# The kept pooled part is added to the gated output by an accumulating transfer on GpSimd's queue

## The chip, the cores and the metric

The kernel runs on one core of one Trainium2 chip. A core has five engines that run side by side and wait for each other through semaphores: TensorE (PE in the profile, with its weight loads as PEld) multiplies matrices into PSUM banks, VectorE (DVE) and ScalarE (ACT) work element by element, GpSimd (POOL) does the same without access to PSUM, and SyncE (SP) issues transfers between the chip's memory and the on-chip SBUF. Each engine runs its own instructions in a fixed order. The metric is the time of one execution on the device in microseconds. Before the change the median of three runs is 1211.2 us (1210.49 to 1212.1).

## The reference

One block of a streaming encoder on 1024 tokens of width 1024, with 16 meta tokens ahead of them, all in float32. A pooling mixer and a gated linear attention work side by side, and their outputs are merged by two sigmoid gates; an output projection and a squared-ReLU MLP follow. Cut to what matters here:

```python
def hybrid_mixer(u, ...):
    z = jnp.einsum('bld,dn->bln', u, w_in)
    a, q, k, v, r, lr, ga, gb = jnp.split(z, IN_SPLITS, axis=-1)
    ...
    y_a = jnp.einsum('blc,cd->bld', p, w_pool_out)
    ...
    y_b = jnp.einsum('blc,cd->bld', o.reshape(B, L, GLA_VAL), w_gla_out)
    m = jax.nn.sigmoid(ga) * y_a + jax.nn.sigmoid(gb) * y_b
    return jnp.einsum('bld,de->ble', m, w_out)
```

Here `p` is the multi-scale pooling of `a` and `o` the output of the linear attention. The change concerns the `+` in `m`: its left side is the pooled part, its right side the gated output of the attention.

## The kernel before

All activations are kept with channels on the 128 partitions and tokens along the free dimension. A tile of 128 channels by 512 tokens (one **half** of the sequence) is the unit of the merge. A float32 product is made of three matmuls of split operands (`mm3`, L281 to L287): each operand is a **high part** (a rounded copy, made by ACT) and a **low part** (what is left, made by DVE). Weights come in through `Raw` buffers by SP and are split the same way in a `Ring` of two slots (L84 on ACT, L85 on DVE).

The stage around the change runs from about 393 to 503 us of the span. Its products are:

- `ya_block(j)`: the pooled product for output channels d = 2j and 2j + 1, both halves. Its gate (a tanh kept in `ga_dram`) is applied by DVE at L1161, and the result is stored in `ma_dram` (L1162). This is the kept pooled part.
- `yb_block(j, h)`: the attention's product for d = 2j and 2j + 1 of half h, four k steps of three matmuls each into one of three PSUM banks (`bank("mm")`). DVE applies the gate from `gb_dram` (L1195, the **gate product**, which is the last reader of the bank) and adds the kept pooled part (L1196, the **add**). ACT writes the high part of half the sum (L1199) and DVE the low part (L1200). These are the inputs of the output projection, `out_tile` (L1362).

TensorE's order is written out by hand. In half 0 the blocks run as j = 0, 1, 2, 3, beside the attention's state work (`across`). In half 1 they run as j = 2, 3, 0, one output tile, j = 1, and then the other output tiles. The weights of j = 2 and 3 stay in the ring from half 0 to half 1 (`KEPT`). The order on DVE, ACT, SP and GpSimd is set by a planner when the kernel is built, from the dependences and from its own estimates of durations; an engine then keeps to that order.

Gates and kept parts are loaded ahead by `ask` into a circle of 128x512 buffers, the same buffers also holding the result in place. `take` hands them to a block. There are ten buffers in the first part of the stage (three of the tile `o`, three of `t1`, four of `c`, `lend("o", "t1", "c")` in `gla_open`) and eight in the second (four of a new `t1`, four of a new `o`). At most two less than all may be in flight:

```python
        while wanted and S["io_live"] < most:
            kind, d, h = wanted[0]
            drams = (ga_dram,) if kind == "a" else (gb_dram, ma_dram)
            if S["io_live"] + len(drams) > len(S["io"]) - 2:
                return
```

The second set is made in `merge_open` (L1313), which gives the first set's memory back:

```python
        left.pop_to(left_m)
        right.pop_to(1)
        S["wo"] = [left.push("wo0", [P, 2, KT, HALF], F32R)]
        ...
        buffer("t1", 4)
        buffer("o", 4)
        lend("t1", "o")
```

In the built program's memory map the old `o` lies at bytes 190336 to 196480 of a partition; the new `t1` lies at 188288 to 196480 and so covers it; the new `o` (from 196480) covers the attention's half 0 output `yg0`; and `wo0` covers the old `c` and `t1`. A tile that is placed over an older one waits until all uses of the whole older tile are over.

`wo` is the split output projection weight. Its first half is loaded into `acc` and split by L1344 (ACT) and L1345 (DVE), and the first output tile reads it.

Of the kernel before, what the change touches and what calls it, by code (L numbers as in the profile page):

```python
# [11 lines left out]
ALU = mybir.AluOpType  # L12
# [110 lines left out]
def kernel(  # L123
# [3 lines left out]
    nc = tc.nc  # L127
# [6 lines left out]
    act, dve, pool, pe = nc.scalar, nc.vector, nc.gpsimd, nc.tensor  # L134
# [19 lines left out]
    def bank(tag):  # L154
        if tag == "sc":
            sc_n[0] += 1
            return two("sc")[:, sc_n[0] % 2]
        return psp[tag].tile([P, 512], F32, name=f"b_{tag}", tag=tag)
# [10 lines left out]
    ma_dram = dp.tile([8, 2, P, HALF], F32, name="ma_dram")  # L169
    gb_dram = dp.tile([8, 2, P, HALF], F32, name="gb_dram")  # L170
    r_dram = dp.tile([HEADS, 2, P, HALF], F32, name="r_dram")
    ga_dram = dp.tile([8, 2, P, HALF], F32, name="ga_dram")
# [38 lines left out]
    def f32(ap):  # L211
        return ap.bitcast(F32)
# [68 lines left out]
    def mm3(ps, n, lhs, rhs, first=True, last=True, more=False):  # L281

        for i in range(n):
            (ah, al), (bh, bl) = lhs(i), rhs(i)
            pe.matmul(ps, ah, bh, start=first and i == 0, stop=False, skip_group_check=more)  # L285
            pe.matmul(ps, ah, bl, start=False, stop=False, skip_group_check=more)  # L286
            pe.matmul(ps, al, bh, start=False, stop=last and i == n - 1, skip_group_check=more)  # L287
# [151 lines left out]
    def first_stage(xs, us, xm, um, lrraw):  # L439
# [23 lines left out]
        def ask(i, j):  # L463
            vraw.append(raw.load(w_rows(C_V + 256 * i, 256, j), D).rearrange("p (k c) -> p k c", k=4))

        ask(0, 0)
        ask(0, 1)
        load(2)
        load(3)
# [79 lines left out]
        def low(i, j):  # L549
# [4 lines left out]
            wait=lambda i, j: W1.ask(),  # L554
            square=square, log=log, exp=exp, root=root, scale=scale, turn=turn, keep=keep, hi=hi, lo=lo, high=high,
            low=low, ask=ask, value=v_half, out=v_out, first=W1.split, meta=lambda t: transposed(um[:META], 0, 0),
        )
        for word in ORDER_1.split():
# [564 lines left out]
    def slot():  # L1123
        S["io_n"] += 1
        return S["io"][(S["io_n"] - 1) % len(S["io"])]

    def ask(most=16):

        while wanted and S["io_live"] < most:
            kind, d, h = wanted[0]  # L1130
            drams = (ga_dram,) if kind == "a" else (gb_dram, ma_dram)
            if S["io_live"] + len(drams) > len(S["io"]) - 2:
                return
            S["io_live"] += len(drams)
            have[wanted.pop(0)] = [slot() for _ in drams]
            for o, dram in zip(have[kind, d, h], drams):
                nc.sync.dma_start(o, dram[d, h])

    def take(*key):
        S["io_live"] -= len(have[key])  # L1140
        return have[key]
# [30 lines left out]
    def yb_block(j, h):  # L1172
        def fn(wb=None):
            if h and j in KEPT:
                wb = kept.pop(j)
            elif j in KEPT:
                kept[j] = wb
            hi, lo = (t.rearrange("p (k c) -> p k c", k=4) for t in wb)
            while not h and ("o", 0) not in done:
                yield "wait"  # L1180
            yg = S["yg"][h]
            for e in range(2):
                d, w = 2 * j + e, slice(e * P, (e + 1) * P)
                ask()
                gl, ml = take("b", d, h)
                b = bank("mm")
                for k in range(4):
                    mm3(
                        b, 1, lambda i: (hi[:, k, w], lo[:, k, w]),
                        lambda i: (yg[:, 0, k], yg[:, 1, k]), first=k == 0, last=k == 3,  # L1190
                    )
                    yield 3 * 512 / 2400
                if e:
                    yield "keep" if j in KEPT and not h else "free"
                dve.scalar_tensor_tensor(gl, gl, 1.0, b, ALU.add, ALU.mult)  # L1195
                dve.tensor_tensor(gl, gl, ml, ALU.add)  # L1196
                th = MH[h][:, d]
                tl = ML[h][:, d]
                act.activation(th, gl, ACT.Copy, scale=0.5)  # L1199
                dve.scalar_tensor_tensor(tl, gl, 0.5, f32(th), ALU.mult, ALU.subtract)  # L1200

        return fn
# [536 lines left out]
```

## Time and profile before

| | |
|---|---|
| median of three runs | 1211.2 us |
| the profiled execution's span | 1209.1 us |
| TensorE busy | 1194.4 us, 99% |
| VectorE busy | 837.5 us, 69% |
| ScalarE busy | 574.4 us, 48% |
| GpSimd busy | 79.1 us, 7% |
| the add, L1196, all 16 | 0.68 us each, 453.0 to 502.7 us |
| transfers that load or store `ma_dram` | 32, to landing 2.7 / 4.8 / 9.0 us (least, median, longest) |

The profile shows one execution, its times counted from the start of the span; the median of the runs is 2.1 us above that span, for what lies around it. A row of the timeline gives start and length in us, engine, line, operation, what is written from what is read, and in brackets how long the engine had stood idle and what ended that. Names in rows are those of the program's tiles without their numbers, so `t` is a buffer of `t1`; `th` and `tl` are high and low parts, `w1h` and `w1l` the ring's split weights, `raw` its loads. SPq is SP's queue of transfers.

### The profile page before, as it was taken

Reading aid. Unit: us, or ns where it says so; the run is one execution under the profiler, and the core shown is the slowest. Engines: PE = TensorE matmul, PEld = TensorE weight load, DVE = VectorE, ACT = ScalarE, POOL = GpSimd, SP = SyncE. Lnnn points to the kernel's source line nnn. Section 1 sums busy time; section 2 is a strip of 40 time slices with the busy share of each in tenths; the row PEclk is TensorE's granted clock in tenths of the full one; section 3 lists DMA queues with packets and bytes.
Section 4 is the critical chain, followed back from the end, with each engine's and each line's share of the span. In section 5 each row is a group of like instructions: output and inputs, shape, how many; then the busy total and the mean of one; then the engine's idle time right before and its main releaser. Section 6 shows DMA issues by size and latency. Waiting matters only on the chain.

```text
span 1209.1 us, 18303 instructions
## 1 busy us (share of the span) xinstructions
PE 1194.4 (99%) x6775; PEld 993.1 (82%) x6775; DVE 837.5 (69%) x1369; ACT 574.4 (48%) x1014; POOL 79.1 (7%) x97
## 2 busy tenths in 40 slices
PE   9999999999999999999999999999999999999997
PEld 7999877878778887788788888888888888888886
DVE  6636567565686669726887767677675887887686
ACT  7546444444456124305655545455464444444554
POOL 0000062323320000000000000000000000000000
PEclk9999999999999999999999999999999999999999
DMA  8223253534348978812255444444479963333532
GB/s 245 77 60 123 91 133 110 166 110 146 112 138 296 315 218 268 284 32 87 88 161 168 151 139 157 148 160 151 152 253 318 348 229 98 98 100 91 173 96 88
DMA packets 151385, 192.79 MB, mean 159 GB/s; under 512 B 12216, under 2 KB 86256, under 8 KB 151296
## 3 DMA queue, kind: packets, MB, share of 16 engines
q1 hardware_dynamic: 151136, 191.56, 49.5%
q8 instruction: 53, 0.87, 0.3%
q14 instruction: 36, 0.29, 0.1%
q10 hardware_dynamic: 160, 0.07, 0.0%
HBM read 128.66 MB, written 62.93 MB: 158 GB/s over the span
## 4 chain that ended last, share of the span: by engine, by line
PE 68%; DVE 3%; issue 1%; DMA 1%; ACT 1%; DVEq 0%; ACTq 0%
PE b_oa L287 5%; PE b_oa L285 5%; PE b_oa L286 5%; PE b_y L285 4%; PE b_y L286 4%; PE b_y L287 4%; PE b_mm L285 4%; PE b_mm L287 4%; PE b_mm L286 4%; PE b_ob L287 4%; PE b_ob L285 4%; PE b_ob L286 4%; PE b_z L286 3%; PE b_z L285 3%; PE b_z L287 3%; PE b_sc L285 2%
## 5 line engine op out<-in xcount | busy, mean ns | idle before, releaser
L774 ACT ACTIVATE w1h<-raw 128x512 fp32r<-128x512 f32 x106 | 65.8, 622 | 51.2 <-PE b_sc L286 21.2
L285 PE MATMUL b_sc<-th,w1h 128*128 128x512 f32 x216 | 85.4, 395 | 0.4 <-ACT u2p L1522 0.4
L285 PE MATMUL b_z<-th,w1h 128*128 128x512 f32 x216 | 84.9, 393 | 0.4 <-DVE c L893 0.4
L775 DVE TENSOR_TENSOR w1l<-raw,w1h 128x512 fp32r<-128x512 f32 x106 | 72.5, 685 | 18.0 <-ACT w1h L774 18.0
L286 PE MATMUL b_sc<-tl,w1h 128*128 128x512 f32 x216 | 84.8, 393 | 0.0
L286 PE MATMUL b_z<-tl,w1h 128*128 128x512 f32 x216 | 84.2, 390 | 0.4 <-DVE tl L1408 0.4
L287 PE MATMUL b_sc<-th,w1l 128*128 128x512 f32 x216 | 84.4, 391 | 0.0
L287 PE MATMUL b_z<-th,w1l 128*128 128x512 f32 x216 | 84.1, 389 | 0.0
L774 ACT ACTIVATE w1h<-fs 128x512 fp32r<-128x512 f32 x81 | 51.1, 630 | 67.0 <-PE b_y L286 33.6
L775 DVE TENSOR_TENSOR w1l<-fs,w1h 128x512 fp32r<-128x512 f32 x81 | 57.7, 712 | 23.7 <-ACT w1h L774 23.7
L285 PE MATMUL b_mm<-th,w1h 128*128 128x512 f32 (+1 forms) x208 | 72.0, 346 | 0.0
L287 PE MATMUL b_mm<-th,w1l 128*128 128x512 f32 (+1 forms) x208 | 71.1, 342 | 0.0
L286 PE MATMUL b_mm<-tl,w1h 128*128 128x512 f32 (+1 forms) x208 | 71.0, 342 | 0.0
L774 ACT ACTIVATE w1h<-bt 128x512 fp32r<-128x512 f32 x46 | 29.1, 632 | 70.8 <-issue 43.9
L1598 DVE TENSOR_TENSOR bt<-w,w 128x512 f32<-128x512 f32 x80 | 54.7, 683 | 2.7 <-DMA w<-in_w_ff_dram 2.7
L285 PE MATMUL b_mm<-wo,th 128*128 128x512 f32 x128 | 50.4, 394 | 0.9 <-PE b_mm L287 0.9
L287 PE MATMUL b_mm<-wo,tl 128*128 128x512 f32 x128 | 49.9, 390 | 0.0
L286 PE MATMUL b_mm<-wo,th 128*128 128x512 f32 x128 | 49.8, 389 | 0.0
L285 PE MATMUL b_y<-wo,w1h 128*128 128x512 f32 x128 | 49.8, 389 | 0.0
L286 PE MATMUL b_y<-wo,w1h 128*128 128x512 f32 x128 | 49.8, 389 | 0.0
L287 PE MATMUL b_y<-wo,w1l 128*128 128x512 f32 x128 | 49.8, 389 | 0.0
L775 DVE TENSOR_TENSOR w1l<-bt,w1h 128x512 fp32r<-128x512 f32 x46 | 31.8, 691 | 25.6 <-ACT w1h L774 25.6
(425 smaller groups left out, 3317.1 us busy)
## 6 DMA issues: line engine op xcount, KB each, us to landing
hf_dram<-h SPq DMA_DIRECT2D x112, 256.0 KB, 2.1
raw<-hf_dram SPq DMA_DIRECT2D x112, 256.0 KB, 2.6
w<-in_w_ff_dram SPq DMA_DIRECT2D x64, 256.0 KB, 4.8
raw<-in_w_in_dram SPq DMA_DIRECT2D x22, 512.0 KB, 4.7
raw<-in_w_ff_dram SPq DMA_DIRECT2D x16, 512.0 KB, 4.1
rawx<-in_w_ff_dram SPq DMA_DIRECT2D x16, 512.0 KB, 4.1
rawp<-in_w_in_dram SPq DMA_DIRECT2D x10, 512.0 KB, 4.2
xs<-in_x_dram SPq DMA_DIRECT2D x8, 512.0 KB, 4.8
```

Source lines behind the costliest of these rows:

```text
L285: pe.matmul(ps, ah, bh, start=first and i == 0, stop=False, skip_group_check=more)
L286: pe.matmul(ps, ah, bl, start=False, stop=False, skip_group_check=more)
L287: pe.matmul(ps, al, bh, start=False, stop=last and i == n - 1, skip_group_check=more)
L774: act.activation(hi, a, ACT.Copy)
L775: dve.tensor_tensor(lo, a, f32(hi), ALU.subtract)
L1598: dve.tensor_tensor(bt, w, S["w2"][q[3:]][:, i], ALU.add if q[2] == "+" else ALU.subtract)
```

## The change

The kept pooled part is not loaded any more. `ask` takes one buffer for a block of kind "b", for the gate alone. After the gate product, GpSimd's queue issues a transfer that reads the kept part from `ma_dram` and adds it to the gate product in place, in SBUF; VectorE's add goes. The high and low part read the buffer as before, now after that transfer.

```diff
         while wanted and S["io_live"] < most:
             kind, d, h = wanted[0]
-            drams = (ga_dram,) if kind == "a" else (gb_dram, ma_dram)
+            drams = (ga_dram,) if kind == "a" else (gb_dram,)
             if S["io_live"] + len(drams) > len(S["io"]) - 2:
                 return
...
                 ask()
-                gl, ml = take("b", d, h)
+                gl, = take("b", d, h)
                 b = bank("mm")
...
                 dve.scalar_tensor_tensor(gl, gl, 1.0, b, ALU.add, ALU.mult)
-                dve.tensor_tensor(gl, gl, ml, ALU.add)
+                nc.gpsimd.dma_start(gl, ma_dram[d, h], accum_op=ALU.add)
                 th = MH[h][:, d]
                 tl = ML[h][:, d]
                 act.activation(th, gl, ACT.Copy, scale=0.5)
```

## The prediction

> **What bounds the kernel now.** I read the page's first two parts, then who waited for whom on PE, and then, because the change lies in one stage, the stretches from 451 to 503 us.
>
> ```profile
> span 1209.1 us, 18303 instructions
> PE 1194.4 (99%) x6775; PEld 993.1 (82%) x6775; DVE 837.5 (69%) x1369; ACT 574.4 (48%) x1014; POOL 79.1 (7%) x97
> ...
> PE b_mm L285 <- DVE o L1195: 0.9, 1, 0.9
> PE b_mm L285 <- PE b_mm L287: 0.9, 1, 0.9
> ...
> PE b_mm L287 <- DVE w1l L85: 0.2, 1, 0.2
> ...
> 461.00:471.00 10.00, 9.85 (x47) 7.91 (x46) 10.00 (x14) 4.35 (x7) 0.00 (x0) 1.00 0.59 184
> 471.00:481.00 10.00, 9.10 (x41) 7.24 (x40) 9.06 (x12) 5.06 (x6) 0.00 (x0) 1.00 0.97 345
> 481.00:491.00 10.00, 9.13 (x40) 7.26 (x40) 8.24 (x12) 3.79 (x5) 0.00 (x0) 1.00 0.87 285
> ```
>
> PE is busy for all but 14.7 us of the span, so DVE's 69% is no bound of the whole. Columns of the stretches: length, then busy time of PE, PEld, DVE, ACT, POOL, granted clock (1.00), DMA share, GB/s. Only here is DVE full (10.0 of 10), and here PE stands still three times: 0.15, 0.90 and 0.87 us, 1.92 us in all. That is the most that this stage can give back, 0.16%. I call a change of 0.2% (2.4 us) about what a measurement of this kernel can tell from none.
>
> I name a block by half and d, so 0.6 is d = 6 of half 0. PE computes 0.0 to 0.7, then 1.4 to 1.7, 1.0, 1.1, an output tile, 1.2, 1.3. Each takes twelve matmuls, 2.7 us, and one of three banks, which its gate product (L1195) frees. What frees the bank for 1.7 is seen in the timelines:
>
> ```profile
> 479.51 0.39 PE L287 MATMUL b_mm<-yg,w1l 128*128 128x512 f32 x1
> 480.80 0.50 PE L285 MATMUL b_mm<-yg,w1h 128*128 128x512 f32 x1 [0.90 <-DVE o L1195]
> 490.12 0.47 PE L285 MATMUL b_mm<-wo,th 128*128 128x512 f32 x1 [0.87 <-PE b_mm L287]
> ...
> 476.06 0.68 DVE L1200 SCALAR_TENSOR_TENSOR tl<-o,th 128x512 fp32r<-128x512 f32 x1
> 480.07 0.68 DVE L1195 SCALAR_TENSOR_TENSOR o<-o,b_mm 128x512 f32<-128x512 f32 x1
> 482.26 0.69 DVE L1195 SCALAR_TENSOR_TENSOR t<-t,b_mm 128x512 f32<-128x512 f32 x1 [1.51 <-DMA t<-gb_dram]
> 489.35 0.68 DVE L1195 SCALAR_TENSOR_TENSOR o<-o,b_mm 128x512 f32<-128x512 f32 x1
> ...
> 471.77 0.34 SPq L1137 DMA_DIRECT2D o<-gb_dram  x1
> 476.77 0.32 SPq L1137 DMA_DIRECT2D t<-gb_dram  x1
> ```
>
> The gate of 1.4 goes into the new tile t1 ("t"), whose memory covers the older stage's tile o. Its load leaves at 476.77, 0.03 after the last low part from o (block 0.7, 476.06 + 0.68). The wait is for the whole tile: t1's first buffer touches no byte of o. It lands for the product at 482.26. PE would have stood longer if the gate of 1.6, in the new tile o (load at 471.77), had not let its product run first, at 480.07, and free a bank. The wait at 490.12 ends with another late gate product, 489.35 + 0.68.
>
> **The change part by part.** It takes 16 adds of L1196 off DVE and 16 loads off SP, gives POOL 16 accumulating transfers, and counts one buffer for a block where it was two.
>
> ```profile
> 471.66 0.68 DVE L1196 TENSOR_TENSOR c<-c 128x512 f32<-128x512 f32 x1
> 472.38 0.63 ACT L1199 ACTIVATE th<-c 128x512 fp32r<-128x512 f32 x1 [1.77 <-DVE c L1196]
> 473.05 0.69 DVE L1200 SCALAR_TENSOR_TENSOR tl<-c,th 128x512 fp32r<-128x512 f32 x1
> ...
> hf_dram<-h SPq DMA_DIRECT2D x112, 256.0 KB, 2.1
> acc<-in_w_out_dram SPq DMA_DIRECT2D x4, 512.0 KB, 7.1
> t<-ma_dram SPq DMA_DIRECT2D x6, 256.0 KB, 3.9
> DMA to landing us min/median/max: 2.7/4.8/9.0
> ```
>
> *Removed.* An add costs 0.68 us, so 16 make 10.9 us of DVE. Almost all of it lies beside PE, so its worth is at most the two bank waits. The loads of the kept part cost SP some 0.3 us of issue each, as the gate's do (476.77), and only the adds waited for them. *POOL's issues* have the queue to themselves: POOL is at 0.00 in every stretch above, so behind a waiting transfer stands only the next one, 2.7 us later. No row shows POOL issuing a transfer; the nearest are SP's issues of 0.32 and 0.34, and I leave it inside L.
>
> *L*, from the end of the gate product to the landing of the sum, takes the place of 0.6 us, and the trace has no accumulating transfer. It reads 256 KB from memory, and reads and writes as many bytes in SBUF. Bounds: 2.1 (a store of that size in a quiet stage) and 9.0 (the slowest ma_dram transfer, the last row above). Between ma_dram's 3.9 in this stage and the 7.1 of 512 KB I take the middle, **5.5**. The Trainium skill (DMA: Bandwidth & Descriptors, Anatomy of one DMA) fits 2.0 us plus bytes over 436 GB/s to a transfer from this queue; that makes an estimate of 2.6 us. By it the sum below would come out at -1.6; plain transfers of that size need longer here, 3.9.
>
> *Moved, first term.* Buffers now go round one by one: 0.0 to 0.3 take c, 0.4 to 0.6 take o, 0.7 takes t1; in half 1 the blocks 1.4 to 1.7 take the four of the new t1 and 1.0 to 1.3 those of the new o. So the first three banks of half 1 all hang on t1, and t1 on the low part of 0.6, which now comes after a transfer:
>
> ```profile
> 469.31 0.39 PE L287 MATMUL b_mm<-yg,w1l 128*128 128x512 f32 x1
> 469.86 0.68 DVE L1195 SCALAR_TENSOR_TENSOR c<-c,b_mm 128x512 f32<-128x512 f32 x1
> ```
>
> The first matmul of 0.7 starts at 468.86, so 0.6 ends at 469.02. DVE, relieved, makes its gate product at once, to 469.8. Landing at 469.8 + L; high and low part 1.40 (472.34 to 473.74 above); gate load at 471.2 + L, landing 5.49 later (476.77 to 482.26); gate product 0.68; PE 0.05 behind (480.75 to 480.80). PE restarts at 477.45 + L. It could start at 479.90, so it stands for **L - 2.45**, in place of 0.90. After that the gates of 1.0 to 1.3 lie long loaded, so the 0.87 goes. Net: L - 2.45 - 0.90 - 0.87 = L - 4.2, at 5.5 **+1.3**, and no less than -1.77.
>
> *Moved, second term.* The high parts wait for transfers on ACT, and behind them stand the weight splits:
>
> ```profile
> 451.40 0.42 SPq L118 DMA_DIRECT2D raw<-in_w_gla_out_dram  x1
> 458.87 0.38 SPq L118 DMA_DIRECT2D raw<-in_w_gla_out_dram  x1
> ...
> 451.32 0.68 DVE L1195 SCALAR_TENSOR_TENSOR c<-c,b_mm 128x512 f32<-128x512 f32 x1
> 453.65 0.68 DVE L1195 SCALAR_TENSOR_TENSOR c<-c,b_mm 128x512 f32<-128x512 f32 x1
> 457.63 1.22 DVE L85 TENSOR_TENSOR w1l<-raw,w1h 128x1024 fp32r<-128x1024 f32 x1
> ...
> 455.75 0.63 ACT L1199 ACTIVATE th<-c 128x512 fp32r<-128x512 f32 x1 [1.36 <-DVE c L1196]
> 456.29 1.04 ACT L84 ACTIVATE w1h<-raw 128x1024 fp32r<-128x1024 f32 x1
> ...
> 466.46 0.50 PE L287 MATMUL b_mm<-yg,w1l 128*128 128x512 f32 x1 [0.15 <-DVE w1l L85]
> ```
>
> This is a chain with no slack: load 451.40, split on ACT 456.29, on DVE 457.63 to 458.85, next load 458.87, and so on to PE's wait at 466.46. If the high part of 0.0 keeps its place ahead of the split, the split starts at 452.0 + L + 0.54 (the step from 455.75 to 456.29), which is L - 3.75 later than 456.29: **+1.75** at 5.5, passed on in full to 466.46 and to everything behind. Ends: 0 if the planner puts it behind the split, and L - 1.4 = 4.1 if the high part of 0.1 (product to 454.33) stands ahead too. The plan isn't in the trace. Today both stand ahead with ACT idle before them, so the nearest case is one that keeps some of that; I take the first.
>
> *Costed at nothing* (first the rows):
>
> ```profile
> 473.82 1.06 ACT L1344 ACTIVATE wo<-acc 128x1024 fp32r<-128x1024 f32 x1 [0.81 <-DVE tl L1200]
> 474.92 1.23 DVE L1345 TENSOR_TENSOR wo<-acc,wo 128x1024 fp32r<-128x1024 f32 x1 [0.58 <-ACT wo L1344]
> ...
> 501.31 0.69 DVE L1195 SCALAR_TENSOR_TENSOR o<-o,b_mm 128x512 f32<-128x512 f32 x1
> 511.99 0.39 PE L285 MATMUL b_mm<-wo,th 128*128 128x512 f32 x1
> ```
>
> The low part of 0.7 also gates wo's tile: 472.5 + L + 1.4 = 479.4, against 473.82 now. Its four splits need at least 1.06 + 4 x 1.23 = 6.0 us, to 485.4, and the output tile starts at 490. Without that cover a DVE split ahead of a gate product costs 1.2 each; two of them are in the range. At the end of the stage 1.3 is ready at 502.0 + L + 1.4 = 508.9, before output tile 4: tile 3 starts at 511.99 and takes 24 matmuls, 5.4 us, so tile 4 starts at 517.4, 8.5 later.
>
> **Sum.** +1.3 + 1.75 = +3.05 on a span of 1209.1: 1212.15. The runs' median of 1211.2 is 2.1 above the span, so 1214.25, about **1214.2**.
>
> **The rivals.**
> - *The transfer is quick (not slower).* POOL's transfers come one at a time, 2.7 us apart, not in bursts as SP's loads do. At L = 2.6 the second term is 0 and the first -1.6: 1209.6. It decides at L = 4, where both terms together are 0. For: 2.1 us in the quiet stage. Against: DMA is 0.59 to 0.97 busy here, and the same bytes need 3.9. By the Trainium skill (the same page, SWDGE vs HWDGE vs iDMA) a DMA engine takes SP's and GpSimd's transfers from different queues by turns, which speaks for this case; no row here shows it.
> - *The planner puts the splits ahead of the high parts.* Then only the first term is left: 1212.5. For: it is free to order ACT and DVE. Against: today's order.
> - *A slow landing.* At L = 9.0: 4.8 + 5.25 = +10, 1221.3. For: a ma_dram transfer took that once. Against: it is the longest of 32.
> - *The new plan takes waits out elsewhere.* PE's 14.7 idle us lie mostly in other stages: past 2.4 us of gain only so, about 1208.
>
> **Chances.** Forecast (0.0 ahead, L 4.2 to 7.5, +0.4 to +7) 0.48; quick 0.26; splits ahead 0.13; slow 0.08; elsewhere 0.05. Slower by over 0.2% needs 2L - 7.95 > 2.4, L above 5.2: about 0.38 of the forecast's 0.48, all of the slow case and a little of the third, 0.48. Faster by over 0.2%: 0.06. Within: 0.46. The range leaves out the slow case, the low tail of the quick one and the last: 1210.0 to 1218.5.
>
> **What would show it.** Right: on SP the first load into t has moved behind the low part of 0.6 and leaves at 476 to 478; PE waits 2 to 4 us before 1.7 and no more at the output tile; ACT waits for POOL's transfer ahead of the split at 456; DVE falls well under 10 between 461 and 471. Wrong: landings under 4 us, or PE without a wait in 451 to 491 (the first term falls), or L84 at 456.3 as before (the second falls). A stall behind 503 us, in a stage that the change doesn't touch, would be the planner's and not of these terms.

## The result, and the profile after

The changed kernel takes 1228.7 us (median of four runs, 1228.4 to 1229.39) where the kernel before, on the same chip, takes 1211.61 (four runs, 1210.49 to 1212.1). The ratio is 1.0149, its 95% interval 1.0135 to 1.0164: slower by about 1.5%, 17.1 us by the medians. On another chip, where the kernel before takes 1209.46, four more runs of the change have a median of 1229.53, and there it is 20.1 us; the loss is 17 to 20 us. The forecast was 1214.2 and its range ended at 1218.5; the sign was right and the size was not.

The page of the changed kernel, its first two parts (busy time, share and count of each engine; then the span in 40 slices):

```profile
span 1227.6 us, 18312 instructions
PE 1201.2 (98%) x6775; PEld 996.9 (81%) x6775; DVE 828.4 (67%) x1353; ACT 574.4 (47%) x1014; POOL 91.7 (7%) x113
...
PE   9999999999999998799999999999999999999997
...
PEclk9999999999999998899999999999999999999999
```

The span is 18.5 us longer. TensorE does the same 6775 matmuls, and yet is busy for 6.8 us more (1194.4 before). Two slices dip, the 16th and 17th of 40 (460 to 522 us), and the granted clock dips in the same two. Who waited for whom on TensorE there (447 to 536 us; us in total, times, longest):

```profile
PE b_mm L285 <- DVE t L1195: 7.9, 3, 6.1
PE b_mm L285 <- ACT w1h L84: 4.6, 2, 3.4
PE b_mm L287 <- DVE w1l L85: 0.8, 2, 0.5
```

That makes 13.3 us of standing still, where the kernel before had 1.92 in the same stage: 11.4 more. With the 6.8 us more of busy time that is 18.2 of the 18.5. The same two sums in stretches (columns as in the prediction: length, busy time of PE, PEld, DVE, ACT, POOL, granted clock, DMA share, GB/s):

```profile
447.00:475.00 28.00, 22.57 (x98) 17.34 (x97) 19.58 (x31) 8.52 (x12) 5.33 (x6) 0.94 0.62 146
475.00:485.00 10.00, 10.00 (x39) 8.10 (x38) 2.61 (x4) 1.26 (x2) 1.72 (x2) 0.84 0.95 256
...
495.00:505.00 10.00, 3.92 (x13) 2.88 (x12) 6.23 (x8) 2.21 (x3) 1.02 (x2) 0.85 0.77 221
505.00:515.00 10.00, 10.00 (x37) 8.07 (x37) 2.68 (x5) 1.89 (x3) 2.46 (x3) 0.80 0.92 207
...
473.00:475.00 2.00, 1.85 (x4) 1.49 (x5) 0.79 (x2) 0.52 (x1) 0.12 (x1) 0.50 0.90 309
475.00:477.00 2.00, 2.00 (x6) 1.59 (x5) 0.00 (x0) 0.00 (x0) 0.00 (x0) 0.50 1.05 254
...
504.00:506.00 2.00, 2.00 (x6) 1.54 (x5) 1.15 (x2) 0.00 (x0) 1.16 (x2) 0.50 0.71 74
506.00:508.00 2.00, 2.00 (x6) 1.59 (x5) 0.00 (x0) 0.63 (x1) 0.59 (x1) 0.50 1.03 249
```

VectorE, full before between 461 and 471, has room everywhere now; what the change took off it is free, and nobody uses it. TensorE is busy for all ten microseconds from 475 and from 505 and still gets 39 and 37 matmuls done there instead of 46 (the kernel before, 495 to 505): behind its long waits it has half the clock. The two-microsecond rows show that clock at 0.50.

Why it waits is read in the timelines of the changed kernel, VectorE, ScalarE and GpSimd beside each other (start, length, engine, line, operation; in brackets the idle time before and what ended it):

```profile
451.40 0.68 DVE L1195 SCALAR_TENSOR_TENSOR c<-c,b_mm 128x512 f32<-128x512 f32 x1
452.40 1.01 POOL L1196 DMA_DIRECT2D c<-ma_dram  x1 [83.42 <-DVE c L1195]
453.29 0.69 DVE L1195 SCALAR_TENSOR_TENSOR c<-c,b_mm 128x512 f32<-128x512 f32 x1
454.28 0.87 POOL L1196 DMA_DIRECT2D c<-ma_dram  x1 [0.87 <-DVE c L1195]
456.97 0.63 ACT L1199 ACTIVATE th<-c 128x512 fp32r<-128x512 f32 x1 [7.86 <-DMA c<-ma_dram]
457.64 0.69 DVE L1200 SCALAR_TENSOR_TENSOR tl<-c,th 128x512 fp32r<-128x512 f32 x1 [3.67 <-ACT th L1199]
458.25 0.68 DVE L1195 SCALAR_TENSOR_TENSOR c<-c,b_mm 128x512 f32<-128x512 f32 x1
459.16 0.63 ACT L1199 ACTIVATE th<-c 128x512 fp32r<-128x512 f32 x1 [1.55 <-DMA c<-ma_dram]
459.69 1.04 ACT L84 ACTIVATE w1h<-raw 128x1024 fp32r<-128x1024 f32 x1
460.79 0.50 PE L285 MATMUL b_mm<-yg,w1h 128*128 128x512 f32 x1 [1.21 <-ACT w1h L84]
...
470.55 1.04 ACT L84 ACTIVATE w1h<-raw 128x1024 fp32r<-128x1024 f32 x1
471.64 0.79 PE L285 MATMUL b_mm<-yg,w1h 128*128 128x512 f32 x1 [3.40 <-ACT w1h L84]
...
485.08 1.74 SPq L1137 DMA_DIRECT2D t<-gb_dram  x4
...
498.84 0.63 ACT L1199 ACTIVATE th<-t 128x512 fp32r<-128x512 f32 x1 [4.38 <-DMA t<-ma_dram]
499.38 1.04 ACT L84 ACTIVATE w1h<-raw 128x1024 fp32r<-128x1024 f32 x1
499.50 0.69 DVE L1200 SCALAR_TENSOR_TENSOR tl<-t,th 128x512 fp32r<-128x512 f32 x1 [3.58 <-ACT th L1199]
501.52 0.69 DVE L1200 SCALAR_TENSOR_TENSOR tl<-t,th 128x512 fp32r<-128x512 f32 x1 [0.19 <-ACT th L1199]
502.13 0.68 DVE L1195 SCALAR_TENSOR_TENSOR t<-t,b_mm 128x512 f32<-128x512 f32 x1
502.87 0.80 PE L285 MATMUL b_mm<-yg,w1h 128*128 128x512 f32 x1 [6.08 <-DVE t L1195]
```

Follow one round. The gate product of 0.0 ends at 452.08, its transfer is issued, and the sum is there at 456.97, when ScalarE makes the high part. VectorE has stood still for 3.67 us, because the next instruction in its order is the low part of that block. Behind it waits the gate product of 0.2 (458.25), whose matmuls need no sum at all; and on ScalarE the weight split (459.69) waits behind the high parts of 0.0 and 0.1. Each landing has become a link in the loop that feeds TensorE: gate product, transfer, high part, low part, next gate product. At 502.13 the same loop, with two landings in a row, gives the longest wait, 6.08 us ahead of block 1.1.

The view of the transfers' own line (who waited for it, us and times; then issue to landing, least, median, longest):

```profile
  ACT th L1199: 57.1, 16
...
DMA to landing us min/median/max: 4.0/5.2/8.3
```

And from ScalarE's timeline of the kernel before, three weight splits that the prediction did not show:

```profile
464.11 1.04 ACT L84 ACTIVATE w1h<-raw 128x1024 fp32r<-128x1024 f32 x1
...
477.21 1.04 ACT L84 ACTIVATE w1h<-raw 128x1024 fp32r<-128x1024 f32 x1
...
485.31 1.05 ACT L84 ACTIVATE w1h<-raw 128x1024 fp32r<-128x1024 f32 x1
```

All 16 high parts waited for a transfer, 57.1 us of idle ScalarE. The weight splits, at 456.29, 464.11, 477.21 and 485.31 before, come at 459.69, 470.55, 490.57 and 499.38: late by 3.4, 6.4, 13.4 and 14.1 us. The delay isn't only passed on; it grows from round to round.

### The profile page after: what moved, and what is told of

It reads as the page before. It is cut to its first block, busy times and chain, and to the rows that moved or that the text cites. A ratio compares the mean times of both kernels' runs of the same rounds, so it can differ in the third digit from the quotient of the medians.

```text
span 1227.6 us, 18312 instructions
## 1 busy us (share of the span) xinstructions
PE 1201.2 (98%) x6775; PEld 996.9 (81%) x6775; DVE 828.4 (67%) x1353; ACT 574.4 (47%) x1014; POOL 91.7 (7%) x113
## 4 chain that ended last, share of the span: by engine, by line
PE 62%; issue 6%; DMA 3%; DVE 2%; ACT 1%; POOL 0%; SPq 0%; POOLq 0%; DVEq 0%
PE b_oa L286 5%; PE b_oa L287 5%; PE b_oa L285 5%; PE b_y L285 4%; PE b_y L287 4%; PE b_y L286 4%; PE b_ob L286 4%; PE b_ob L285 4%; PE b_ob L287 4%; PE b_mm L285 3%; PE b_mm L286 3%; PE b_mm L287 3%; PE b_z L286 3%; PE b_z L285 3%; PE b_z L287 3%
```

## The experiments

The theory at the start: the order on VectorE and ScalarE puts each landing in front of the next block's work (**order**). Rivals: the tile wait of the prediction's first term, through the count of buffers (**tile**); the accumulation being slow in itself (**transfer**). Times below are medians; the ratio is to the kernel before on the same chip, with its interval. The change itself did not run on the chip of the first four runs, so what they take back is compared with its loss on two other chips, 17 to 20 us.

**What is there to gain: no add at all.** This kernel leaves the kept part out: neither loaded nor added.

```diff
-                nc.gpsimd.dma_start(gl, ma_dram[d, h], accum_op=ALU.add)
```

> Leaves out the kept pooled part: no load, no add, no transfer; everything else as in the changed kernel. It is the floor of what the change could give. Order theory (the landing stands in the chain of ACT and DVE, and weight splits and gate products queue behind it): with the transfer gone all of the loss goes, 1209 to 1212 us, and PE shows no half clock in 447 to 535 us. Buffer theory (one buffer a block makes the first three gates of half 1 hang on the old tile o): PE still waits 2 us or more ahead of block 1.7, 1213 us or more. Transfer theory (the accumulating transfer itself is slow): also 1209 to 1212.

1208.06 us, ratio 0.9986 (0.9976 to 0.9995); TensorE waits for nothing between 447 and 540. So the most that any way of moving the add can bring is 1.6 us. The change costs 17 to 20 to win at most that.

**Two buffers for a block again.** The second buffer stays empty, so the buffers go round as in the kernel before.

```diff
-            drams = (ga_dram,) if kind == "a" else (gb_dram,)
+            drams = (ga_dram,) if kind == "a" else (gb_dram, None)
...
-                gl, = take("b", d, h)
+                gl, _ = take("b", d, h)
```

> The changed kernel, with two buffers taken for a block as before the change; the second is left unused. Order theory: within 4 us of the changed kernel, 1225 to 1232. Buffer theory: most of the loss goes, 1216 or less. Transfer theory: no change, 1225 to 1232.

1231.29 us, 1.0179 (1.0163 to 1.0196). The waits for splits stay, 1.32, 0.53, 1.53 and 0.78 us, a gate product makes TensorE stand for 6.55, and an output tile for 4.15. The buffer count is not the cause.

**A plain copy in place of the accumulation**, on the same queue. The sum isn't formed: the buffer ends up holding the kept part.

```diff
-                nc.gpsimd.dma_start(gl, ma_dram[d, h], accum_op=ALU.add)
+                nc.gpsimd.dma_start(gl, ma_dram[d, h])
```

> The same transfer on GpSimd's queue, but as a plain copy over the gate product (so the sum is not formed). Order theory: any transfer at this place costs the same, 1223 to 1231, its landing 4.5 us or more in the median against 5.2. Transfer theory: landing falls to 3 us or less and the time to 1218 or less. Buffer theory: as the changed kernel.

1222.01 us, 1.0103 (1.0088 to 1.0118). GpSimd issues a copy in 0.54 us (0.86 with accumulation), and from there to the landing:

```profile
DMA to landing us min/median/max: 2.8/3.9/6.5
```

1.3 us less in the median than in the change's profile, and still 12.4 of the 17 to 20 us stay, with a wait of 5.13 us on a gate product. Accumulating is a part of the price, and most of the price comes without it. Time and landing came out between the two forecasts, just below what order theory had given. The 1.3 is rough: in the second run of the change the accumulating transfers' median is 6.6 us, in the run with two buffers 4.8.

**The parts later.** Each block's high and low part are put two blocks later, in a fixed place behind the gate product of the block that is then done; the transfers are as in the change.

```diff
+    LAG, owing = 2, []
+
+    def parts_due(most):
+        while len(owing) > most:
+            gl, th, tl = owing.pop(0)
+            tc.keep_in_program_order(act.activation(th, gl, ACT.Copy, scale=0.5))
+            tc.keep_in_program_order(dve.scalar_tensor_tensor(tl, gl, 0.5, f32(th), ALU.mult, ALU.subtract))
...
                 nc.gpsimd.dma_start(gl, ma_dram[d, h], accum_op=ALU.add)
-                th = MH[h][:, d]
-                tl = ML[h][:, d]
-                act.activation(th, gl, ACT.Copy, scale=0.5)
-                dve.scalar_tensor_tensor(tl, gl, 0.5, f32(th), ALU.mult, ALU.subtract)
+                owing.append((gl, MH[h][:, d], ML[h][:, d]))
+                parts_due(LAG)
+            if not h and j == 3:
+                parts_due(0)
...
     step(rest, out_tile(1, 0))
+    step(rest, lambda: parts_due(0))
```

> The changed kernel with the high and low part of a block written two blocks later and pinned there in the order of ACT and DVE; the last two of half 0 at once after its last block, the last two of half 1 after the next output tile. Order theory: PE's waits for the weight splits (5.4 us) go, with one of the two stretches at half clock (3.3 us), and the wait ahead of block 1.7 shrinks to L - 2.45 = 2 to 4 us: 1212 to 1218. Buffer theory: 1222 or more, since the old tile o is read to its end even later. Transfer theory: 1222 or more.

1216.55 us, 1.0057 (1.0042 to 1.0072): 10 of the 17 us are gone (13 of 20 by the other chip), and no weight split is waited for any more. The transfers did not get quicker for it, their median is 7.5 us to landing here. TensorE's two waits that are left, in its timeline, and the load behind the first:

```profile
483.13 0.80 PE L285 MATMUL b_mm<-yg,w1h 128*128 128x512 f32 x1 [3.66 <-DVE t L1203]
495.33 0.47 PE L285 MATMUL b_mm<-wo,th 128*128 128x512 f32 x1 [1.19 <-issue]
...
478.84 0.69 DVE L1176 SCALAR_TENSOR_TENSOR tl<-o,th 128x512 fp32r<-128x512 f32 x1 [1.28 <-ACT th L1175]
...
479.56 1.75 SPq L1137 DMA_DIRECT2D t<-gb_dram  x4
```

(L1203 is the gate product here, L1176 the low part.) Here the prediction's first term shows up alone: the low part of 0.6 ends at 479.53, the gate load of half 1 leaves 0.03 us later, and TensorE stands for that gate product, with 6.8 us of half clock from 481.8 on.

**The parts later, and the second buffer set begun with the new `o`**, to take the tile wait away as well; and the same turn of buffers in the change and in the kernel before:

```diff
-        lend("t1", "o")
+        lend("o", "t1")
```

> The kernel of e4_late_parts, and the second set of buffers begins with the new tile o, so that the first four gates of half 1 no longer hang on the last reader of the old o. If e4's remaining loss (a wait of 3.66 us ahead of block 1.7 and the half clock behind it) comes from that tile wait, both go: 1208 to 1211. If it comes from late landings through the order of ACT and DVE, PE still waits in half 1: 1213 or more.

> The changed kernel with only that order of the buffers turned round. Order theory (the changed kernel's waits in half 1 come from gate products that stand behind low parts on DVE): most of the loss stays, 1219 to 1228. Buffer theory: 1216 or less.

> The kernel before, with the order of the buffers turned round. If its own wait of 0.90 us ahead of block 1.7 is the tile wait, that wait shrinks or goes: 0.3 to 1.8 us faster than before. If DVE's load sets it, no difference within 0.5 us.

In the kernel before, the turn does nothing to the time: 1210.04, 1.0003 (0.9994 to 1.0012); one wait of 1.70 us at 486.31 stands in place of the two of 0.90 and 0.87. In the change, nothing either: 1229.02, 1.0158 (1.0144 to 1.0172). With later parts it gives 1218.74, 1.0068 (1.0055 to 1.0081), no better than without. Its gate loads leave at 470.99, but on VectorE:

```profile
478.38 0.69 DVE L1176 SCALAR_TENSOR_TENSOR tl<-o,th 128x512 fp32r<-128x512 f32 x1 [5.79 <-ACT th L1175]
...
480.98 0.68 DVE L1203 SCALAR_TENSOR_TENSOR o<-o,b_mm 128x512 f32<-128x512 f32 x1
```

The tile wait went, and the queue behind a low part took its place: the gate product stood behind half 0's last parts, which waited 5.79 us for a landing.

**The change once more**, on that chip, as a measure of how well runs agree:

> The changed kernel once more, beside the others on one chip: 1.0149 of before again, within 0.0015. PE stands still for more than 3 us at a time in one or more places, and each such place is followed by 5 to 7 us at half clock.

1229.53 us, 1.0165 (1.0151 to 1.0179). The median agrees with the first four runs within a microsecond, the ratio lies just above what was expected, since the kernel before is quicker on this chip. Single waits differ between two executions (3.34 us in place of 1.23 before 1.7), and behind that 3.34 there were 3.4 us of half clock, not the 5 to 7 expected.

**No transfer, but GpSimd's own add**, in two pieces, with the kept part loaded as before:

```diff
-                dve.tensor_tensor(gl, gl, ml, ALU.add)
+                for c in (slice(0, 256), slice(256, 512)):
+                    pool.tensor_tensor(gl[:, c], gl[:, c], ml[:, c], ALU.add)
```

> The kernel before, its 16 adds made by GpSimd on the SBUF operands (two halves of 256 columns) instead of VectorE; loads and buffers as before. It takes the same work off VectorE, but the sum is there some 2 to 3 us after the gate product, and not 5 to 8. Order theory (it is the late landing that holds ACT and DVE): 1207 to 1212, no stretch at half clock. If any hop through GpSimd's queue in this chain were the trouble: 1216 or more.

A miss: 1218.32 us, 1.0071 (1.0059 to 1.0084), where 1207 to 1212 was expected. The hop is only some 1.5 to 2.4 us, and costs 8.6:

```profile
451.38 0.68 DVE L1195 SCALAR_TENSOR_TENSOR c<-c,b_mm 128x512 f32<-128x512 f32 x1
...
454.27 0.69 DVE L1201 SCALAR_TENSOR_TENSOR tl<-c,th 128x512 fp32r<-128x512 f32 x1 [1.08 <-ACT th L1200]
454.88 0.68 DVE L1195 SCALAR_TENSOR_TENSOR c<-c,b_mm 128x512 f32<-128x512 f32 x1
457.77 0.69 DVE L1201 SCALAR_TENSOR_TENSOR tl<-c,th 128x512 fp32r<-128x512 f32 x1 [2.21 <-ACT th L1200]
458.38 0.68 DVE L1195 SCALAR_TENSOR_TENSOR o<-o,b_mm 128x512 f32<-128x512 f32 x1
```

The planner put each low part (L1201) straight ahead of the next gate product, so the gate products come every 3.50 us, while TensorE makes a block in 2.7. That the hop was short didn't matter; it had to be shorter than what the order left for it.

**The half clock by itself.** The kernel before, with TensorE held once, by ScalarE copies in front of a transpose, in a place that has nothing to do with the change; two copies, then eight (the diff shows the first; the second has `range(7)`).

```diff
+            if (t, ch) == (5, 0):
+                hold = S["u2"][:, 0, :HALF]
+                act.activation(hold, S["acc"][:, 4, :HALF], ACT.Copy)
+                for _ in range(1):
+                    act.activation(hold, hold, ACT.Copy)
+                pe.transpose(bank("ms")[:, :P], hold[:, :P], ident)
```

> The kernel before, with one deliberate hold of PE in a quiet stage: ahead of output tile 5 it waits for a chain of two copies on ACT that begins when tile 4 is added. PE stands still about 2 us. If a short gap costs only itself, the time grows by that gap plus 0.1 of a transpose, 2 to 2.5 us, and the granted clock stays 1.00.

> As e10, with eight copies: PE stands still about 5.5 us. Clock theory (a gap over some 3 us brings 3 to 6.5 us at half clock behind it): the time grows by the gap plus 1.7 to 3.3 us, 7.2 to 8.8 in all, with rows of clock 0.50 behind the gap. If the half clock in the changed kernel had another cause: 5.5 to 6 us, clock 1.00.

The long hold: a wait of 6.07 us, 1218.95, 9.2 more than the 1209.75 of the kernel before. The short one, timeline and then stretches:

```profile
524.60 0.33 PE L1375 MATMUL b_ms<-ident,u 128*128 128x128 f32 x1 [2.11 <-ACT u L1374]
```

```profile
526.00:528.00 2.00, 2.00 (x6) 1.53 (x5) 0.00 (x0) 0.00 (x0) 0.00 (x0) 0.50 0.03 8
528.00:530.00 2.00, 2.00 (x7) 1.59 (x6) 0.00 (x0) 0.00 (x0) 0.00 (x0) 0.66 0.00 0
```

1213.41 (1212.06 to 1215.24), 3.7 more, for a wait of 2.11. No half clock was expected behind so short a wait, and there were 3.4 us of it, by the two rows: a miss, and a wait's price is here itself plus some 1.5 us, the long one's itself plus 3.

**GpSimd's add with later parts**, two blocks and then one. The first gives buffers back too early, so that its late parts may read what a later load has put there (another sum); the second counts them until the low part is issued.

```diff
     def take(*key):
-        S["io_live"] -= len(have[key])
+        if key[0] == "a":
+            S["io_live"] -= 1
         return have[key]
...
-    LAG, owing = 2, []
+    LAG, owing = 1, []
...
             gl, th, tl = owing.pop(0)
+            S["io_live"] -= 2
```

> The kernel of e9 (GpSimd makes the adds) with the high and low parts two blocks later and pinned, as in e4. If e9's loss comes from the order alone (on VectorE the low part of a block stands ahead of the next gate product, and now waits for a hop of 2 us), it goes: 1207 to 1211, no half clock, no wait of PE for a weight split. If work on GpSimd itself holds VectorE up, 1214 or more.

> The kernel before, with its sixteen adds made by GpSimd as in the run where they cost 7 us more, but with the high and low part of each block put one block later, and a block's two buffers given back only when its low part is issued, so that the sums are those of the reference. Theory that the order on VectorE and ScalarE alone makes the loss (a low part that waits for the sum stands ahead of the next gate product): with the parts a block later the gate product waits for nothing of GpSimd's, and the time is that of the kernel before: 1207.5 to 1211 us on a chip where that takes 1210, TensorE waiting under 2 us in the stage. Rival, the slow hop itself or GpSimd's use of SBUF beside VectorE makes it: 1214 or more. Third: one block of delay (2.7 us of TensorE's work) is too little for a hop of 1.4 to 2.4 us plus two parts, and some 1 to 3 us of waits stay: 1211 to 1213.

1209.81, ratio 1.0 (0.9991 to 1.0009), and 1211.53, 1.0015 (1.0006 to 1.0024). The hop is the one that cost 8.6 us (the 7 in the expectation are too few); with the parts behind the next gate products it costs 0 and 1.7. This is the order theory's test without any transfer. It holds for the greater part, but not in full with one block: the third case came, with one wait of 2.55 us left. That wait ends with the first gate product of half 1, a gate load that left at 477.09 behind the low part of 0.7. (Later parts gain 1.7 us by themselves, as the control below shows; against that control the hop costs 3.3 with one block.)

**What stays with later parts of the change.** Blocks 0.6 and 0.7, then 0.4 to 0.7, load their kept part as before; the others accumulate, parts two blocks later. The second also counts a block's buffers until its low part is issued, which the first does not; so two things differ between them.

```diff
-            drams = (ga_dram,) if kind == "a" else (gb_dram,)
+            drams = (ga_dram,) if kind == "a" else (gb_dram,) if h or d < 6 else (gb_dram, ma_dram)
...
-                nc.gpsimd.dma_start(gl, ma_dram[d, h], accum_op=ALU.add)
+                if ml:
+                    dve.tensor_tensor(gl, gl, ml[0], ALU.add)
+                else:
+                    nc.gpsimd.dma_start(gl, ma_dram[d, h], accum_op=ALU.add)
```

> The kernel of the change with the high and low parts two blocks later (6.9 us over the kernel before), but blocks 0.6 and 0.7 load their kept part and have it added by VectorE as before, so that half 1's first gate products do not stand behind a landing. Theory that the 6.9 us left are these two landings, ahead of half 1's gate products on VectorE and of its gate loads: 1208.5 to 1212 us, TensorE's wait of 3.66 us at 483 under 1 us and no half clock behind it. Rival, another wait (the output tile's, the weight's splits, or transfers of the other blocks) makes them: 1215 or more.

> As the run with blocks 0.6 and 0.7 loaded and the parts two blocks later, but 0.4 to 0.7 load their kept part and have it added by VectorE. In that run the sum of 0.5 left at 468.68 behind three 512 KB loads of the output weight (467.25) and was read at 477.86, some 9 us later, and the gate loads of half 1, which wait for the low part of 0.5 in the old tile, left at 479.84. Theory that what stays of the loss is this: transfers that share the queues with the output weight's loads, in front of half 1's gate loads. Without them the gate loads leave before 477, TensorE's wait of 4.0 us is under 1, and the time is 1208.5 to 1212 us where the kernel before takes 1210. Rival, the weight of half 1's own transfers or the output tile's wait makes it: 1214 or more.

The first: 1216.79, 1.0058 (1.0044 to 1.0072), a miss; not those two landings. Its timeline says which:

```profile
468.68 0.86 POOL L1207 DMA_DIRECT2D o<-ma_dram  x1 [1.88 <-DVE o L1203]
...
477.86 1.15 ACT L1175 ACTIVATE th<-o 128x512 fp32r<-128x512 f32 x2 [4.66 <-DMA o<-ma_dram]
```

The sum of 0.5 takes 9.2 us from issue to use. It was issued 1.4 us after three 512 KB loads of the output weight (467.25 on SP's queue); that these made it slow is argued, no run moves them alone. The old `o` waits for the low parts of 0.5 and of 0.6 right behind it (478.52 to 479.81), and the gate load leaves at 479.84. The second: 1212.87, 1.0029 (1.0018 to 1.004), just above what was expected. The wait before 1.7 falls from 3.97 to 0.49 us, and one of 2.74 is left at the first output tile (490.52). It ends as the gate product at 489.74 does, which stands on VectorE behind a weight split, and that on ScalarE behind the high part of 1.4 at 486.98, 7.7 us after its gate product: half 1's own landings in the loop. So what stays has, as far as these two runs go, two parts: the tile wait, and a loop that two blocks are too few for when a transfer needs over 7 us.

**The control: later parts in the kernel before**, with VectorE's add and no transfer; one block later.

```diff
                 dve.tensor_tensor(gl, gl, ml, ALU.add)
-                th = MH[h][:, d]
...
+                owing.append((gl, MH[h][:, d], ML[h][:, d]))
+                parts_due(LAG)
```

> The kernel before with its high and low parts one block later and nothing else changed: what the later parts do by themselves. If they are neutral, the runs with later parts show what the transfers cost: 1208.5 to 1211 us. If they cost or gain by themselves (gate loads of half 1 that leave later, since the low parts come later; the two waits of 0.9 us taken away), 1212 or more, or 1208 and less.

1208.26 us, 0.9987 (0.9979 to 0.9996), and in its profile:

```profile
span 1206.5 us, 18301 instructions
...
479.31 0.50 PE L285 MATMUL b_mm<-yg,w1h 128*128 128x512 f32 x1 [0.63 <-DVE t L1205]
```

It beats both kernels, and reaches what the kernel without any add reached (0.9986). The little that the stage could give back came from the order of VectorE and ScalarE, with every add still on VectorE.

## Why the prediction was wrong

**The bound** was read rightly: at most some 2 us to win (1.6 measured), TensorE full.

**L was right, the number of times it was paid was not.** Taken as 5.5 with ends 2.1 and 9.0; from the end of the gate product to the high part it was 4.9 for 0.0 (452.08 to 456.97), 5.2 for 0.1, and over the sixteen blocks 4.3 to 8.7 with a median of 5.7. In the second run's profile the landings are slower (median from issue 6.6 in place of 5.2), at the same total time.

**The second term is the step that failed:** "If the high part of 0.0 keeps its place ahead of the split", L - 3.75 = +1.75, "passed on in full to 466.46 and to everything behind". The first split came 3.4 late, near the 4.1 of that term's own upper end, as 0.1 stood ahead too. But the step treats the delay as paid once, at the first block. The planner left a high part ahead of a split and a low part ahead of a gate product again and again, and each round adds its own delay: 3.4, 6.4, 14.1 us at the splits. Today's order was quoted as the reason for the choice; the same order at the other fifteen blocks was not followed. The gate products of 0.0 and 0.7 lie 20.9 us apart in the kernel before (451.32 and 472.26) and 29.4 after (451.40 and 480.82): 8.5 us were lost before half 1 began. Moving the parts away takes 10 of 17 us back (13 of 20), with the same transfers.

The sum that was missing is an inequality. From one gate product over transfer, high and low part (1.4) to the gate product behind it (0.7) it takes L + 2 us or a little more; if k blocks of TensorE's work, 2.7 each, lie between, the loop holds TensorE up once L + 2 passes 2.7 k. An estimate by it: with k = 1 at most 0.7 us of hop are free, with k = 2 3.4, with k = 3 6.1. It sorts the runs: GpSimd's add at k = 1 costs 8.6 us, at k = 2 1.7 (and that by another wait), at k = 3 nothing; a plain copy at 3.9 plus its issue costs at the planner's mix of k = 1 and 2; half 1's 7.7 us costs even at k = 3.

**The half clock is the term that was left out.** 6.8 of the 18.2 us are longer busy time, and some 6 of them are matmuls at a clock of 0.50 behind waits (an estimate: two stretches of 6.8 us each, TensorE idle for 1.4 of them, half of the rest lost). Neither sum nor range had it; the forecast's wait of 2 to 4 us was counted as costing only itself, and the holds show that 2.11 us can cost more.

**The first term** named a true mechanism, and not the one that decided. The load into `t` left 0.03 us behind the last low part of the old `o` in the kernel before, and leaves at 485.08 after (476 to 478 was expected); but it is late because the whole loop is, and turning the buffers changes nothing. Only with the loop loosened does it show: a gate load at 479.56 against 471.2 + L = 479.8 to 480.1 at that run's 8.6 (from the issue) to 8.9 (from the gate product's end), and a wait of 3.66 rather than L - 2.45 = 6.2, since the load itself took 2.8 us and not 5.49. Before 1.7, where 2 to 4 us were expected, TensorE stood for 1.23. "The 0.87 goes" came true to the letter, nothing was waited for at the output tile (508.15); but a block earlier, ahead of 1.1, came the 6.08 us at 502.87, the loop again.

**Costed at nothing**: TensorE didn't wait at the output tile, as predicted, and the stage explains 18.2 of the 18.5 us, so nothing was lost behind it. **VectorE** fell to 6.7 of 10 between 461 and 471. **Slow landing**, the worst rival (1221.3 at L = 9), is still 7 us short: with delays counted once, no L within the bounds gives this time. The range varied the transfer and hardly the plan.

## What to carry to other kernels

Before a cheap in-order instruction is replaced by a transfer, look at what stands behind its readers on each engine, and compare the new latency with the work that the bounding engine has left before it needs those followers, block by block: a delay inside a loop is paid in every round. If a latency must go in, move its readers behind the next rounds' work first; here that alone was worth more than the change could ever bring. And add the clock to every wait of TensorE that reaches some 2 us, alone or in two pieces close together.

## What the runs showed of the hardware

- **The clock falls behind short waits.** Single waits of 0.90, 1.21 and 1.70 us left the clock whole; one of 2.11, those of 2.55 and 2.60 and all longer ones were followed by half clock. Length alone doesn't decide: with two buffers for a block, waits of 1.32 and 0.53 us with 0.7 us of matmuls between them brought 3.4 us at 0.50, and so did 1.51 and 0.78 in the plain copy's run, while 1.16 and 1.31 did not in the run of GpSimd's add. Every stretch of half clock was 3.4, 6.8 or, once, 10.2 us long, and with two buffers the four began at 461.92, 472.16, 489.22 and 519.94, whole multiples of 3.41 us apart; so it seems to matter where a wait falls on such a grid, which no run tests. The Trainium skill (TensorE: Matmul & The Clock Gate, Why this matters for your kernels) puts the limit at gaps above about 3 us; here less was enough.
- **An accumulating transfer on GpSimd's queue** of 256 KB took 0.86 us to issue in the median; from issue to landing its median was 4.8 to 7.7 us over the runs that have it (5.2 and 6.6 in two runs of the same kernel), its least 3.9 and its longest 10.9. A plain copy there took 0.54 and, in its one run, 3.9. The estimate of 2.6 us that the prediction worked out from the fit in the Trainium skill (DMA: Bandwidth & Descriptors, Anatomy of one DMA) was not reached by any of them; the fastest plain copy took 2.8.
- **GpSimd's add** of 128x256 took 0.73 us in most cases, and up to 1.72. A pair of them took 2.3 us beside a weight split or L1273 on VectorE, which read two tiles in SBUF, and 1.44 beside L1265, which reads a PSUM bank.
